# Four pairs instead of three by seven products in the second part's down, and an earlier product with A12, in a decoder block's feed-forward networks

## The chip, the cores and the metric

The kernel runs on one core of a Trainium2 chip, in one launch. The metric is the device time of that launch in microseconds (us). Engines are named as in the profile: TensorE (PE, with its weight loads as PEld), VectorE (DVE), ScalarE (ACT), GpSimd (POOL) and SyncE (SP).

## The reference

One block of a hybrid decoder for 256 tokens, model width 2048, in float32. Cut to what matters here:

```python
def swiglu(x, w_gu, w_down):
    gate, up = jnp.split(x @ w_gu, 2, axis=-1)
    return (jax.nn.silu(gate) * up) @ w_down

h = h + 0.5 * swiglu(rms_norm(h, ffn1_norm), ffn1_w_gu, ffn1_w_down)
h = h + hybrid_mixer(rms_norm(h, mix_norm), ...)
h = h + 0.5 * swiglu(rms_norm(h, ffn2_norm), ffn2_w_gu, ffn2_w_down)
gate = jax.nn.sigmoid(rms_norm(h, ple_norm) @ ple_w_gate)
h = h + gate * (p @ ple_w_proj)
return rms_norm(h, final_norm)
```

The hidden width of both feed-forward networks (FFN1 and FFN2) is 5632. The change touches these two alone.

## The kernel before, in words

**Products of two numbers each.** Every matrix product is taken in float32r with operands split in two, a high part and a low one: high by high, high by low, low by high, so three matmuls of 128 x 128 by 512 columns where one would stand. A weight arrives as `raw`; ScalarE casts it (`whi`, L77) and VectorE subtracts (`wlo`, L78). A "pair" is 256 rows of weights by 512 columns, with three buffers for `whi` and `wlo` and four for `raw`. `next_weights` (L82 to L96) runs two pairs and one weight sum ahead of TensorE.

**Parts and groups.** An FFN has its 5632 hidden columns in eleven blocks of 512, in parts of three, four and four blocks (`PARTS`). A part runs one group for the gate and up of each of its blocks (banks g0, g1, u0, u1), and then two down groups, each for two of the four output blocks (banks d0, d1, d0, d1). A down group of part two or three has eight pairs for each output block, and part one's has six.

**Seven products.** A part of each group's pairs, `ns` of them, isn't multiplied plainly (L550 to L552) but by Strassen and Winograd's scheme: with 2 x 2 blocks, the input's A11 to A22 and the weights' quarters, seven products of sums take the place of eight. A pair costs 24 matmuls plainly in a group and 21 by seven products (`product`, L324 to L352: 3 x `ns` matmuls in each of the seven, L342 to L344). The tuple `NS_DOWN` holds `ns` for the down groups of the three parts, 2, 3 and 3 before; `NS` is 4 for gate and up.

- Weight quarters lie in four buffers named R, loaded by a queue of GpSimd (L279). Sums of quarters are made by VectorE (`add`, L307) or by a load that adds (`add_loaded`, L314). Each product's weights are cast by ScalarE (`shi`, L298) and subtracted by VectorE (`slo`, L299); `shi` and `slo` have **two buffers** each. Their width is 512 x `ns`: 1536 elements at three pairs, 2048 at four.
- Input sums come from `halves` (L420 to L471): VectorE adds high and low (S, L456), makes four sums (L462), ScalarE casts (Sh, L464), VectorE subtracts (Sl, L465). Products 0, 4 and 6 take A11, A12 and A22 as they are and need none of it.
- Products 0 and 1 end with a copy of their bank on ScalarE (L347), products 2 and 3 with a copy (`part`, L350) and a subtraction on VectorE (L352).

**The order.** `plan` (L362 to L412) lays the seven products of a group between the plain pairs of the group ahead of it, beginning behind the second or third pair, one product for each further pair. The order of the seven is `SEVEN`, 0, 1, 2, 4, 3, 5, 6; the prediction counts by place, so that "the fifth product" is the fifth one in that order. The work beside the matmuls (`down_input`, L473 to L505: gate by up, a transposition by VectorE and a trip through memory, the cast hTh L504 and the subtraction hTl L505) goes in steps behind each pair (`lanes`). The tile scheduler has the last word on the order on each engine, so a product may come apart and stand between plain matmuls.

Of the kernel before, what the change touches and what calls it, by code (L numbers as in the profile page):

```python
# [27 lines left out]


NS = 4  # L30
NS_DOWN = tuple(3 if i1 - i0 == 4 else 2 for i0, i1 in PARTS)


SEVEN = (0, 1, 2, 4, 3, 5, 6)


W_IN_ORDER = (2, 0, 4, 3, 1, 5, 8, 10, 12, 9, 11, 13, 6, 7)
# [9 lines left out]
def block_kernel(ctx, tc, a, out):  # L47
# [15 lines left out]
    lanes = Lanes(4)  # L63
# [184 lines left out]
    class Group:  # L248
# [8 lines left out]
        def __init__(self, kind, part, src, quarters, ns, bank, nb=0):  # L257
            self.kind, self.part, self.src, self.ns, self.nb, self.bank = kind, part, src, ns, nb, bank
            self.quarters, self.raw, self.first = quarters, {}, False
            self.last = part == len(PARTS) - 1  # L260
            self.banks = self.follower = None
            self.plain = [(b, g) for b in range(2) for g in range(ns, len(src[0]))]
            if kind == "dn" and nb == 0:

                self.plain.sort(key=lambda x: x[1] >= len(src[0]) - 2)
            elif kind == "behind":

                self.plain.sort(key=lambda x: x[1] // 2)
            self.sums = self.all_sums()
# [20 lines left out]
        def all_sums(self):  # L290

            fp = current[0]

            def halved(j, b):
                w = self.raw[j, b]
                hi = fp.tile([P, NS, NB], F32R, tag="shi", name="shi", bufs=2)[:, 0:self.ns]
                lo = fp.tile([P, NS, NB], F32R, tag="slo", name="slo", bufs=2)[:, 0:self.ns]
                keep(nc.scalar.copy(hi, w))  # L298
                nc.vector.tensor_tensor(out=lo, in0=w, in1=hi, op=ALU.subtract)  # L299
                return hi, lo  # L300

            def keep(ins):

                return tc.keep_in_program_order(ins) if self.first == "2" else ins

            def add(x, y):
                keep(nc.vector.tensor_tensor(out=self.raw[x], in0=self.raw[x], in1=self.raw[y], op=ALU.add))  # L307

            def add_loaded(x, y):


                if self.first:
                    return add(x, y)
                nc.gpsimd.dma_start(out=self.raw[x], in_=self.quarters[y[1]][y[0]], accum_op=ALU.add)  # L314

            for i in SEVEN:
                ws = halved(*((0, 0), (0, 0), (0, 0), (0, 1), (1, 0), (1, 1), (0, 0))[i])
                if i == 0:
                    add((0, 0), (0, 1))
                    add_loaded((0, 1), (1, 1))  # L320
                elif i == 1:
                    add((0, 0), (1, 1))
                elif i == 2:
                    add_loaded((0, 0), (1, 0))  # L324
                yield ws
# [28 lines left out]
    def plan(n):  # L354
# [9 lines left out]
        for p, (i0, i1) in enumerate(PARTS):  # L364
            for i in range(i0, i1):
                plain = PLAIN[n]
                if i < plain:
                    src = [([a[f"w_gu{n}0"][2 * i + b][g] for g in range(KD // 2)], None) for b in range(2)]
                else:
                    src = [sources("w_gu" + n, 2 * (i - plain) + b) for b in range(2)]  # L370
                groups.append(Group("gu", p, [x[0] for x in src], [x[1] for x in src], NS if i >= plain else 0,
                                    len(groups) % 2))
            for nb in (0, 2):
                src = [sources(f"w_down{n}{p}", nb + b) for b in range(2)]
                groups.append(Group("dn", p, [x[0] for x in src], [x[1] for x in src], NS_DOWN[p], len(groups) % 2, nb))
        if n == "2":
            src = [sources("w_behind", b) for b in range(2)]
            groups.append(Group("behind", len(PARTS), [x[0] for x in src], [x[1] for x in src], NS_BEHIND,
# [44 lines left out]
    def halves(kind, his, los, ns, wait=0, at_once=2):  # L423
# [19 lines left out]
        for g0 in range(0, ns, at_once):  # L443
            n = min(at_once, ns - g0)
            k0 = 2 * (g0 % 2)
            hi, lo = (x[g0 // 2][:, k0:k0 + 2 * n] for x in (his, los))
            keep = lambda ins: ins
            if g0 == 2 and n == 1:

                keep = tc.keep_in_program_order  # L450
                yield
            if n == 2:
                x = fp.tile([P, 2 * NB], F32, tag="sil", name="S")
            else:
                x = act.tile([P, NB], F32, tag="nat", name="S", bufs=4)
            keep(nc.vector.tensor_tensor(out=x, in0=hi.bitcast(F32).rearrange("p k x -> p (k x)"),  # L456
                                         in1=lo.bitcast(F32).rearrange("p k x -> p (k x)"), op=ALU.add))
            xv = x.rearrange("p (g j t y) -> p g j t y", g=n, j=2, t=2)
            a11, a12, a21, a22 = (xv[:, :, j, t, :] for t in range(2) for j in range(2))
            for o, y, z, op in ((a22, a21, a22, ALU.subtract), (a21, a11, a21, ALU.subtract),  # L460
                                (a11, a22, a11, ALU.subtract), (a12, a11, a12, ALU.add)):
                nc.vector.tensor_tensor(out=o, in0=y, in1=z, op=op)  # L462
            sx = [y[:, g0:g0 + n].rearrange("p g j t y -> p (g j t y)") for y in (sh, sl)]
            nc.scalar.copy(sx[0], x)  # L464
            nc.vector.tensor_tensor(out=sx[1], in0=x, in1=sx[0], op=ALU.subtract)  # L465
            if not g0 % 2 + n == 1 or g0 + n == ns:
                yield

    def ffn(n, nT, r, scale, next_norm, stat):
        xs = picker(*nT)  # L470
        late = callable(r)  # L471
        with tc.tile_pool(name="ffn", bufs=1) as fp:
# [43 lines left out]
            for group, todo in ffn_plan[n]:  # L516
# [5 lines left out]
                if dn and group.nb and not group.last:  # L522
                    lanes.add(1, halves("gu", *nT, NS))
                elif dn and group.nb and group.follower:
                    lanes.add(1, halves("behind", *nxt, NS_BEHIND, 4))
                elif not dn and group.follower.kind == "dn" and not group.part:
                    lanes.add(1, halves("dn", hTh[i0:], hTl[i0:], NS_DOWN[group.part]))
                if dn and group.last and nxt is None:
                    nxt = new_nT()
                if group.banks is None:  # L530
# [1 line left out]
                for kind, one in todo:  # L532
                    if kind == "seventh":
                        follower = group.follower
                        follower.product(SEVEN[one])
                        if group.part and not dn and one == 5 and follower.kind == "gu" and \
                                follower.follower.kind == "dn":
                            p = PARTS[group.part][0]
                            lanes.add(1, halves("dn", Later(hTh, p), Later(hTl, p), NS_DOWN[group.part], 0, 1))
                        continue  # L540
                    b, g = one
                    whi, wlo = next_weights()
# [29 lines left out]
                    else:  # L572
# [7 lines left out]
                        hTl.append(tl)  # L580
                        i0, i1 = PARTS[group.part]

                        last = (3 if i1 - i0 == 4 else 2) if len(hTh) == i1 else 0
                        gen = down_input(outs, sil, th, tl, last)
                        next(gen)

# [762 lines left out]
def _layout(i):  # L1349
    f = {k: np.asarray(v) for k, v in i.items()}  # L1350
    m = {}
# [5 lines left out]
    for n in "12":  # L1357
# [4 lines left out]
        _parted(m, f"w_gu{n}", b[2 * PLAIN[n]:], NS)  # L1362
        b = _blocks(f[f"ffn{n}_w_down"][0])
        for p, (i0, i1) in enumerate(PARTS):
            _parted(m, f"w_down{n}{p}", b[:, 2 * i0:2 * i1], NS_DOWN[p])
    _parted(m, "w_behind", _blocks(f["ple_w_gate"][0])[0:2], NS_BEHIND)
    w = f["w_in"][0]
    m["w_in"] = _blocks(np.concatenate([w[:, :4096], w[:, 4112:]], axis=1))
# [29 lines left out]
```

## Time and profile before

| | us |
|---|---|
| three runs, median | 1944.74 (1944.4 to 1944.83) |
| the profiled execution | 1945.28 |
| its span, first to last instruction | 1943.6 |
| TensorE busy in it | 1928.1 (99%) |
| VectorE busy | 1570.4 (81%) |
| ScalarE busy | 1164.1 (60%) |
| granted TensorE clock, mean | 0.999 |

In a group's row stand line, engine, operation and tile, the shape, the count, then busy time and mean ns of one, then the idle time of the engine just ahead of it with what ended most of it. In a row of the waits stand the waiting instruction, what it waited for, the sum, the times and the longest. In a row of the timeline stand start, duration, engine, line and instruction. A matmul's record runs from issue to its end and overlaps the next one's.

### The profile page before, as it was taken

Reading aid. Unit: us, or ns where it says so; the run is one execution under the profiler, and the core shown is the slowest. Engines: PE = TensorE matmul, PEld = TensorE weight load, DVE = VectorE, ACT = ScalarE, POOL = GpSimd, SP = SyncE. Lnnn points to the kernel's source line nnn. Section 1 sums busy time; section 2 is a strip of 40 time slices with the busy share of each in tenths; the row PEclk is TensorE's granted clock in tenths of the full one; section 3 lists DMA queues with packets and bytes.
Section 4 is the critical chain, followed back from the end, with each engine's and each line's share of the span. In section 5 each row is a group of like instructions: output and inputs, shape, how many; then the busy total and the mean of one; then the engine's idle time right before and its main releaser. Section 6 shows DMA issues by size and latency. Waiting matters only on the chain.

```text
span 1943.6 us, 24163 instructions
## 1 busy us (share of the span) xinstructions
PE 1928.1 (99%) x8884; PEld 1594.0 (82%) x8884; DVE 1570.4 (81%) x1703; ACT 1164.1 (60%) x1362; POOL 148.4 (8%) x226
## 2 busy tenths in 40 slices
PE   9999999999999999999999999999999999999998
PEld 7888888888888888878788888888888888888886
DVE  7879878997789766797856579899888987888865
ACT  6656666666666557664555456566556755657654
POOL 0010110000010000010100000010000100001000
PEclk9999999999999999999999999999999999999999
DMA  8778898888888765556565776788888987989764
GB/s 307 269 236 282 252 293 285 237 288 249 280 285 242 228 218 171 176 169 211 161 213 159 244 283 231 226 281 289 248 275 241 327 264 244 271 237 314 234 214 143
DMA packets 144182, 475.05 MB, mean 244 GB/s; under 512 B 19648, under 2 KB 47296, under 8 KB 129856
## 3 DMA queue, kind: packets, MB, share of 16 engines
q1 hardware_dynamic: 107200, 302.16, 44.4%
q0 software_dynamic: 25920, 160.44, 30.2%
q10 hardware_dynamic: 10944, 10.91, 1.8%
q8 instruction: 69, 1.13, 0.2%
q14 instruction: 49, 0.40, 0.1%
HBM read 451.44 MB, written 22.02 MB: 244 GB/s over the span
## 4 chain that ended last, share of the span: by engine, by line
PE 92%; DVE 5%; DMA 2%; issue 1%; ACT 0%; POOL 0%; SPq 0%; POOLq 0%; DVEq 0%; ACTq 0%
PE d L550 5%; PE d L552 5%; PE d L551 5%; PE u L551 5%; PE u L552 5%; PE u L550 5%; PE g L343 5%; PE g L342 5%; PE g L344 5%; PE g L551 4%; PE g L552 4%; PE pj L112 4%; PE pj L113 4%; PE pj L114 4%; PE g L550 4%; PE d L344 3%
## 5 line engine op out<-in xcount | busy, mean ns | idle before, releaser
L77 ACT CAST whi<-raw 128x1024 fp32r<-128x1024 f32 (+1 forms) x489 | 511.3, 1049 | 401.1 <-PE pj L114 106.6
L78 DVE TENSOR_TENSOR wlo<-raw,whi 128x1024 fp32r<-128x1024 f32 (+1 forms) x489 | 592.0, 1218 | 162.9 <-ACT whi L77 161.8
L299 DVE TENSOR_TENSOR slo<-R,shi 128x2048 fp32r<-128x2048 f32 (+2 forms) x224 | 444.9, 1989 | 132.1 <-ACT shi L298 130.1
L298 ACT CAST shi<-R 128x2048 fp32r<-128x2048 f32 (+2 forms) x224 | 373.9, 1671 | 141.5 <-DVE R L307 62.7
L112 PE MATMUL pj<-whi,nTh 128*128 128x512 f32 x448 | 179.4, 401 | 0.0
L113 PE MATMUL pj<-wlo,nTh 128*128 128x512 f32 x448 | 175.2, 391 | 1.1 <-DVE wlo L78 1.1
L114 PE MATMUL pj<-whi,nTl 128*128 128x512 f32 x448 | 174.9, 390 | 0.0
L550 PE MATMUL d<-whi,hTh 128*128 128x512 f32 x448 | 174.5, 390 | 0.0
L551 PE MATMUL d<-wlo,hTh 128*128 128x512 f32 x448 | 174.4, 389 | 0.0
L552 PE MATMUL d<-whi,hTl 128*128 128x512 f32 x448 | 173.4, 389 | 0.0
L551 PE MATMUL g<-wlo,nTh 128*128 128x512 f32 x400 | 156.6, 391 | 0.6 <-DVE wlo L78 0.6
L552 PE MATMUL g<-whi,nTl 128*128 128x512 f32 x400 | 156.0, 390 | 0.0
L551 PE MATMUL u<-wlo,nTh 128*128 128x512 f32 x400 | 155.8, 389 | 0.2 <-DVE wlo L78 0.2
L552 PE MATMUL u<-whi,nTl 128*128 128x512 f32 x400 | 155.6, 389 | 0.0
L550 PE MATMUL g<-whi,nTh 128*128 128x512 f32 x400 | 155.0, 391 | 0.6 <-ACT nTh L161 0.6
L550 PE MATMUL u<-whi,nTh 128*128 128x512 f32 x400 | 153.4, 389 | 0.0
L307 DVE TENSOR_TENSOR R<-R 128x2048 f32<-128x2048 f32 (+2 forms) x68 | 135.7, 1996 | 0.1
L113 PEld LDWEIGHTS pj<-wlo,nTh 128*128 128x128 f32 x448 | 84.2, 188 | 18.9 <-DVE wlo L78 2.7
L550 PEld LDWEIGHTS d<-whi,hTh 128*128 128x128 f32 x448 | 84.1, 188 | 18.1 <-ACT hTh L504 1.0
L552 PEld LDWEIGHTS d<-whi,hTl 128*128 128x128 f32 x448 | 84.1, 188 | 17.8
L114 PEld LDWEIGHTS pj<-whi,nTl 128*128 128x128 f32 x448 | 84.1, 188 | 17.6
L551 PEld LDWEIGHTS d<-wlo,hTh 128*128 128x128 f32 x448 | 84.1, 188 | 17.4
(332 smaller groups left out, 3447.0 us busy)
## 6 DMA issues: line engine op xcount, KB each, us to landing
raw<-in_w_gu SPq DMA_DIRECT2D x199, 512.0 KB, 5.8
raw<-in_w_down SPq DMA_DIRECT2D x112, 512.0 KB, 6.4
raw<-in_w_in SPq DMA_DIRECT2D x112, 512.0 KB, 3.4
R<-in_w_gu2q POOLq DMA_DIRECT2D x54, 1024.0 KB, 8.6
R<-in_w_gu1q POOLq DMA_DIRECT2D x48, 1024.0 KB, 8.3
raw<-in_w_out SPq DMA_DIRECT2D x32, 512.0 KB, 4.3
tT<-scr SPq DMA_DIRECT2D x22, 512.0 KB, 5.8
R<-in_w_down11q POOLq DMA_DIRECT2D x12, 768.0 KB, 7.0
```

The source lines that it names most:

```text
L77: nc.scalar.copy(hi[:, j, :], raw[:, j, :])
L78: nc.vector.tensor_tensor(out=lo[:, j, :], in0=raw[:, j, :], in1=hi[:, j, :], op=ALU.subtract)
L112: nc.tensor.matmul(outs[t], xh[:, c], whi[:, j, :], start=st, stop=False)
L113: nc.tensor.matmul(outs[t], xh[:, c], wlo[:, j, :], start=False, stop=False)
L114: nc.tensor.matmul(outs[t], xl[:, c], whi[:, j, :], start=False, stop=sp)
L298: keep(nc.scalar.copy(hi, w))
L299: nc.vector.tensor_tensor(out=lo, in0=w, in1=hi, op=ALU.subtract)
L307: keep(nc.vector.tensor_tensor(out=self.raw[x], in0=self.raw[x], in1=self.raw[y], op=ALU.add))
L344: nc.tensor.matmul(out, xl, whi[:, g, :], start=False, stop=sp, skip_group_check=True)
L550: nc.tensor.matmul(out, xh[:, c], whi[:, j, :], start=st, stop=False, skip_group_check=True)
L551: nc.tensor.matmul(out, xh[:, c], wlo[:, j, :], start=False, stop=False, skip_group_check=True)
L552: nc.tensor.matmul(out, xl[:, c], whi[:, j, :], start=False, stop=sp, skip_group_check=True)
```

## The change

`NS_DOWN` gets a number for each of the two down groups of a part: (2, 2), (4, 4) and (3, 3). So both down groups of part two, in both FFNs, take four of their eight pairs by seven products instead of three; the weights in memory are laid out to match (one array for each group). `SEVEN_DOWN` is a second order, 0, 4, 1, 2, 3, 5, 6, used where the first down group of parts two and three follows the last gate and up: the product with A12, number 4, comes second instead of fourth. The steps of `halves` and `down_input` are fitted to four pairs.

```diff
...
 
 
 NS = 4
-NS_DOWN = tuple(3 if i1 - i0 == 4 else 2 for i0, i1 in PARTS)
+NS_DOWN = (2, 2), (4, 4), (3, 3)
 
 
 SEVEN = (0, 1, 2, 4, 3, 5, 6)
+SEVEN_DOWN = (0, 4, 1, 2, 3, 5, 6)
 
 
 W_IN_ORDER = (2, 0, 4, 3, 1, 5, 8, 10, 12, 9, 11, 13, 6, 7)
...
         def __init__(self, kind, part, src, quarters, ns, bank, nb=0):
             self.kind, self.part, self.src, self.ns, self.nb, self.bank = kind, part, src, ns, nb, bank
             self.quarters, self.raw, self.first = quarters, {}, False
+            self.seven = SEVEN_DOWN if kind == "dn" and part and nb == 0 else SEVEN
             self.last = part == len(PARTS) - 1
             self.banks = self.follower = None
             self.plain = [(b, g) for b in range(2) for g in range(ns, len(src[0]))]
...
                     return add(x, y)
                 nc.gpsimd.dma_start(out=self.raw[x], in_=self.quarters[y[1]][y[0]], accum_op=ALU.add)
 
-            for i in SEVEN:
+            for i in self.seven:
                 ws = halved(*((0, 0), (0, 0), (0, 0), (0, 1), (1, 0), (1, 1), (0, 0))[i])
                 if i == 0:
                     add((0, 0), (0, 1))
...
                 groups.append(Group("gu", p, [x[0] for x in src], [x[1] for x in src], NS if i >= plain else 0,
                                     len(groups) % 2))
             for nb in (0, 2):
-                src = [sources(f"w_down{n}{p}", nb + b) for b in range(2)]
-                groups.append(Group("dn", p, [x[0] for x in src], [x[1] for x in src], NS_DOWN[p], len(groups) % 2, nb))
+                src = [sources(f"w_down{n}{p}{nb // 2}", b) for b in range(2)]
+                groups.append(Group("dn", p, [x[0] for x in src], [x[1] for x in src], NS_DOWN[p][nb // 2],
+                                    len(groups) % 2, nb))
         if n == "2":
             src = [sources("w_behind", b) for b in range(2)]
             groups.append(Group("behind", len(PARTS), [x[0] for x in src], [x[1] for x in src], NS_BEHIND,
...
             k0 = 2 * (g0 % 2)
             hi, lo = (x[g0 // 2][:, k0:k0 + 2 * n] for x in (his, los))
             keep = lambda ins: ins
-            if g0 == 2 and n == 1:
+            if g0 >= 2 and n == 1:
 
                 keep = tc.keep_in_program_order
-                yield
+                if g0 == 2:
+                    yield
             if n == 2:
                 x = fp.tile([P, 2 * NB], F32, tag="sil", name="S")
             else:
...
                 elif dn and group.nb and group.follower:
                     lanes.add(1, halves("behind", *nxt, NS_BEHIND, 4))
                 elif not dn and group.follower.kind == "dn" and not group.part:
-                    lanes.add(1, halves("dn", hTh[i0:], hTl[i0:], NS_DOWN[group.part]))
+                    lanes.add(1, halves("dn", hTh[i0:], hTl[i0:], NS_DOWN[group.part][0]))
                 if dn and group.last and nxt is None:
                     nxt = new_nT()
                 if group.banks is None:
...
                 for kind, one in todo:
                     if kind == "seventh":
                         follower = group.follower
-                        follower.product(SEVEN[one])
+                        follower.product(follower.seven[one])
                         if group.part and not dn and one == 5 and follower.kind == "gu" and \
                                 follower.follower.kind == "dn":
                             p = PARTS[group.part][0]
-                            lanes.add(1, halves("dn", Later(hTh, p), Later(hTl, p), NS_DOWN[group.part], 0, 1))
+                            lanes.add(1, halves("dn", Later(hTh, p), Later(hTl, p), NS_DOWN[group.part][0], 0, 1))
                         continue
                     b, g = one
                     whi, wlo = next_weights()
...
                         hTl.append(tl)
                         i0, i1 = PARTS[group.part]
 
-                        last = (3 if i1 - i0 == 4 else 2) if len(hTh) == i1 else 0
+                        last = (6 - NS_DOWN[group.part][0] if i1 - i0 == 4 else 2) if len(hTh) == i1 else 0
                         gen = down_input(outs, sil, th, tl, last)
                         next(gen)
 
...
         _parted(m, f"w_gu{n}", b[2 * PLAIN[n]:], NS)
         b = _blocks(f[f"ffn{n}_w_down"][0])
         for p, (i0, i1) in enumerate(PARTS):
-            _parted(m, f"w_down{n}{p}", b[:, 2 * i0:2 * i1], NS_DOWN[p])
+            for j in range(2):
+                _parted(m, f"w_down{n}{p}{j}", b[2 * j:2 * j + 2, 2 * i0:2 * i1], NS_DOWN[p][j])
     _parted(m, "w_behind", _blocks(f["ple_w_gate"][0])[0:2], NS_BEHIND)
     w = f["w_in"][0]
     m["w_in"] = _blocks(np.concatenate([w[:, :4096], w[:, 4112:]], axis=1))
```

The rows below are those of FFN1's part two, in program order, with a number behind each tile's name. Lines in the changed kernel are one to five higher than before.

VectorE between the second and the third product, before: `slo_2728` is the second product's, `slo_2793` the third's, `R` the quarter sums, `sil` to `tb` the transposition, `S` input sums, and `wlo` plain pairs of the last gate and up.

```order
L299 TENSOR_TENSOR slo_2728<-R_2548,shi_2727 128x1536
L487 STREAM_TRANSPOSE tb_2744<-sil_2526 128x4x128
L307 TENSOR_TENSOR R_2548<-R_2548,R_2625 128x1536
L487 STREAM_TRANSPOSE tb_2744<-sil_2526 128x4x128
L78 TENSOR_TENSOR wlo_2749<-raw_2747,whi_2748 128x1024
L456 TENSOR_TENSOR S_2770<-hTh_2382,hTl_2383 128x512
L299 TENSOR_TENSOR slo_2793<-R_2548,shi_2792 128x1536
L462 TENSOR_TENSOR S_2770<-S_2770 128x128
L78 TENSOR_TENSOR wlo_2799<-raw_2797,whi_2798 128x1024
```

And now, where `slo_2728` is the product with A12:

```order
L301 TENSOR_TENSOR slo_2728<-R_2633,shi_2727 128x2048
L491 STREAM_TRANSPOSE tb_2743<-sil_2526 128x4x128 x2
L79 TENSOR_TENSOR wlo_2748<-raw_2746,whi_2747 128x1024
L460 TENSOR_TENSOR S_2769<-hTh_2382,hTl_2383 128x512
L301 TENSOR_TENSOR slo_2803<-R_2548,shi_2802 128x2048
L466 TENSOR_TENSOR S_2769<-S_2769 128x128
L309 TENSOR_TENSOR R_2548<-R_2548,R_2625 128x2048
L466 TENSOR_TENSOR S_2769<-S_2769 128x128
L79 TENSOR_TENSOR wlo_2809<-raw_2807,whi_2808 128x1024
```

The wide addition of R has moved behind the third product's slo, ahead of the last row's wlo.

ScalarE at the fourth to seventh products, before (d0 and d1 are banks, `shi_2974` is the first product of the second down group, the others are the first group's):

```order
L298 CAST shi_2825<-R_2633 128x1536
L350 COPY part_2859<-d1_2779 128x512
L298 CAST shi_2862<-R_2584 128x1536
L77 CAST whi_2902<-raw_2901 128x1024
L77 CAST whi_2940<-raw_2939 128x1024
L77 CAST whi_2960<-raw_2959 128x1024
L298 CAST shi_2895<-R_2625 128x1536
L350 COPY part_2930<-d1_2779 128x512
L298 CAST shi_2933<-R_2548 128x1536
L298 CAST shi_2974<-R_2866 128x1536
L504 CAST hTh_2701<-tT_2919 128x4x4x32 x2
```

And now, with `shi_2876` the fifth product, `shi_2915` the sixth, `shi_2956` the seventh and `shi_3000` the first of the second down group:

```order
L468 CAST Sh_2683<-S_2777 128x512
L349 COPY d1_2788<-d0_2787 128x512
L300 CAST shi_2876<-R_2584 128x2048
L352 COPY part_2912<-d1_2786 128x512
L300 CAST shi_2915<-R_2625 128x2048
L78 CAST whi_2983<-raw_2982 128x1024
L78 CAST whi_3035<-raw_3034 128x1024
L352 COPY part_2953<-d1_2786 128x512
L300 CAST shi_2956<-R_2548 128x2048
L300 CAST shi_3000<-R_2880 128x2048
L508 CAST hTh_2701<-tT_2939 128x4x4x32 x2
```

The copy of the bank d0 stands ahead of the fifth product's cast, and two wide casts stand behind each other at the end.

TensorE at the first product of the second down group (bank `d1_3061`), before: the rows ahead of it are plain pairs of the first down group, and 16 rows lie between the end of the seventh product (`shi_2933`) and the second group's first.

```order
L551 MATMUL d1_2779<-wlo_2941,hTh_2382 128x512
L552 MATMUL d1_2779<-whi_2940,hTl_2383 128x512
L550 MATMUL d0_2778<-whi_2960,hTh_2701 128x512
L551 MATMUL d0_2778<-wlo_2961,hTh_2701 128x512
L550 MATMUL d1_2779<-whi_2960,hTh_2701 128x512
L551 MATMUL d1_2779<-wlo_2961,hTh_2701 128x512
L342 MATMUL d1_3061<-shi_2974,hTh_2085 128x512
L343 MATMUL d1_3061<-slo_2975,hTh_2085 128x512
L344 MATMUL d1_3061<-shi_2974,hTl_2086 128x512
```

And now (bank `d1_3090`), with `shi_2915` the sixth product and `shi_2956` the seventh:

```order
L346 MATMUL d0_2787<-shi_2915,Sl_2684 128x512
L344 MATMUL d0_2787<-shi_2915,Sh_2683 128x512
L345 MATMUL d0_2787<-slo_2916,Sh_2683 128x512
L346 MATMUL d0_2787<-shi_2915,Sl_2684 128x512
L344 MATMUL d1_2786<-shi_2956,hTh_2085 128x512
L344 MATMUL d1_3090<-shi_3000,hTh_2085 128x512
L345 MATMUL d1_2786<-slo_2957,hTh_2085 128x512
L346 MATMUL d1_2786<-shi_2956,hTl_2086 128x512
L344 MATMUL d1_2786<-shi_2956,hTh_2085 128x512
L345 MATMUL d1_2786<-slo_2957,hTh_2085 128x512
L346 MATMUL d1_2786<-shi_2956,hTl_2086 128x512
```

The first matmul of the second group stands one matmul behind the end of the sixth product, inside the seventh; the rest of that product follows behind the seventh.

## The prediction

> **What bounds the kernel now.** I read the page's busy times first, then the chain that ended last, then all that TensorE waited for.
>
> ```profile
> span 1943.6 us, 24163 instructions
> PE 1928.1 (99%) x8884; PEld 1594.0 (82%) x8884; DVE 1570.4 (81%) x1703; ACT 1164.1 (60%) x1362; POOL 148.4 (8%) x226
> PE 92%; DVE 5%; DMA 2%; issue 1%; ACT 0%; POOL 0%; SPq 0%; POOLq 0%; DVEq 0%; ACTq 0%
> PE g L551 <- DVE wlo L78: 0.6, 2, 0.4
> PE u L343 <- DVE slo L299: 0.3, 1, 0.3
> PE u L551 <- DVE wlo L78: 0.2, 1, 0.2
> ```
>
> TensorE is the bound. In the FFNs its waits for weights come to 1.1 us in all, so a matmul that goes is a gain in full, and a weight that comes late is a loss in full. The price of a matmul comes from a stretch without a wait:
>
> ```profile
> 300.16 0.39 PE L550 MATMUL g<-whi,nTh 128*128 128x512 f32 x1
> ...
> 304.92 0.39 PE L550 MATMUL g<-whi,nTh 128*128 128x512 f32 x1
> ```
>
> In the kernel's order these two are 21 matmuls apart, and 4.76/21 = 0.2267 us. The record's 0.39 is one matmul from issue to end.
>
> Last I looked at the stretch the change touches, part two's down of FFN1. The windows show, in this order, the pass from gate/up to the first down group, from there to the second, and on to the next gate/up (columns: window and its length, PE, PEld, DVE, ACT, POOL busy, clock, DMA share, GB/s):
>
> ```profile
> 337.00:376.00 39.00, 39.00 (x173) 32.06 (x172) 35.30 (x43) 23.79 (x27) 3.96 (x6) 1.00 0.80 239
> 376.00:413.00 37.00, 37.00 (x165) 30.61 (x165) 35.14 (x34) 25.19 (x26) 3.96 (x6) 1.00 0.97 322
> 413.00:451.00 38.00, 38.00 (x168) 31.06 (x167) 34.87 (x31) 21.26 (x18) 2.88 (x4) 1.00 0.81 244
> ```
>
> VectorE is idle there for 3.70, 1.86 and 3.13 us only, and the DMA engines are at 0.97 in the middle. TensorE never waits, but its cover is thin.
>
> **The change part by part.** Prices of what grows and of what goes (groups, with the mean ns of one behind the busy time):
>
> ```profile
> L299 DVE TENSOR_TENSOR slo<-R,shi 128x2048 fp32r<-128x2048 f32 x133 | 304.4, 2290 | 112.7 <-ACT shi L298 111.9 <-DMA raw<-in_w_gu 0.6
> L299 DVE TENSOR_TENSOR slo<-R,shi 128x1536 fp32r<-128x1536 f32 x56 | 97.9, 1754 | 10.3 <-ACT shi L298 10.1
> L307 DVE TENSOR_TENSOR R<-R 128x2048 f32<-128x2048 f32 x42 | 95.7, 2280 | 0.1
> L307 DVE TENSOR_TENSOR R<-R 128x1536 f32<-128x1536 f32 x16 | 27.9, 1746 | 0.0
> L78 DVE TENSOR_TENSOR wlo<-raw,whi 128x1024 fp32r<-128x1024 f32 x487 | 590.6, 1220 | 160.2 <-ACT whi L77 159.1
> L298 ACT CAST shi<-R 128x2048 fp32r<-128x2048 f32 x133 | 254.3, 1913 | 104.1 <-DVE R L307 53.7 <-PE g L344 27.2 <-PE u L344 21.2
> L298 ACT CAST shi<-R 128x1536 fp32r<-128x1536 f32 x56 | 83.0, 1482 | 21.9 <-PE d L344 8.4 <-PE g L344 6.8 <-PE u L344 6.7
> ```
>
> *1. Matmuls.* Four down groups (two per FFN) take one pair more by seven products: each loses 24 plain matmuls and gains 21. That is 4 x 3 = 12 fewer, 12 x 0.2267 = **-2.72 us**. The Trainium skill ("TensorE: Matmul & The Clock Gate", Part 1, on the 56 ns gap) has 215.7 ns between warm matmuls of 512 columns; by it the gain would be 2.59; the trace's 226.7 decides.
>
> Eight raw pairs go too (per FFN four subtractions, 4.9 us of VectorE). What comes per FFN: 14 wide slo for narrow ones, 14 x 0.536 = 7.5, four wide adds, 4 x 0.534 = 2.1, and one more set of input sums, about 2.5 by its rows:
>
> ```profile
> L462 DVE TENSOR_TENSOR S<-S 128x128 f32<-128x128 f32 x48 | 12.9, 290 | 0.1
> L456 DVE TENSOR_TENSOR S<-hTh,hTl 128x512 f32<-128x512 f32 x12 | 8.3, 688 | 0.0
> L465 DVE TENSOR_TENSOR Sl<-S,Sh 128x512 fp32r<-128x512 f32 x12 | 8.3, 691 | 2.7 <-ACT Sh L464 2.7
> ```
>
> (four of the first, one of each other.) So VectorE takes on 7.2 us net per FFN in a stretch with 8.7 us idle. Averages don't say what is late; the single hand-overs do. These show how fast one engine follows another:
>
> ```profile
> 374.46 0.39 PE L344 MATMUL d<-shi,Sl 128*128 128x512 f32 x1
> 374.88 1.49 ACT L298 CAST shi<-R 128x1536 fp32r<-128x1536 f32 x1 [2.12 <-PE d L344]
> ...
> 370.80 0.59 ACT L350 COPY part<-d 128x512 f32<-128x512 f32 x1 [0.78 <-PE d L344]
> 371.28 1.48 ACT L298 CAST shi<-R 128x1536 fp32r<-128x1536 f32 x1
> 372.80 1.76 DVE L299 TENSOR_TENSOR slo<-R,shi 128x1536 fp32r<-128x1536 f32 x1 [0.27 <-ACT shi L298]
> ```
>
> ScalarE starts 0.03 to 0.04 behind a matmul's end (374.85), a copy holds it 0.48 before the next cast, VectorE starts 0.04 behind the cast. Products have two shi and two slo buffers: a product's cast waits for the last matmul of the product two before it. With ns at four, this chain grows by 0.43 + 0.54.
>
> *2. The pair behind the third product* (its wlo is used at 357.23 in before):
>
> ```profile
> 337.23 1.76 DVE L299 TENSOR_TENSOR slo<-R,shi 128x1536 fp32r<-128x1536 f32 x1 [0.50 <-ACT shi L298]
> 338.91 0.29 DVE L462 TENSOR_TENSOR S<-S 128x128 f32<-128x128 f32 x1
> ...
> 352.21 1.19 DVE L78 TENSOR_TENSOR wlo<-raw,whi 128x1024 fp32r<-128x1024 f32 x1
> 355.78 1.23 DVE L78 TENSOR_TENSOR wlo<-raw,whi 128x1024 fp32r<-128x1024 f32 x1
> ```
> ```profile
> 353.45 0.50 PE L551 MATMUL g<-wlo,nTh 128*128 128x512 f32 x1
> 357.23 0.39 PE L551 MATMUL u<-wlo,nTh 128*128 128x512 f32 x1
> ```
>
> VectorE starts an instruction 0.08 before the record ahead ends (338.91 against 338.99), and works without a gap of note from 337.23 to 357.01. In the changed order it has ahead of that wlo three wide slo and two wide adds (3 x 0.536 + 2 x 0.534), an input sum of 0.60 fewer and one of 0.20 more: +2.28. Its start moves by the wider cast, 0.43. So the wlo ends at 359.72 and TensorE could go on at 359.77. TensorE gets there nine matmuls later, 2.04, less the 0.11 by which its record at 353.45 is longer than 0.39 (a wait that goes): 359.16. Wait **0.61** (0.2 to 0.8, by what VectorE makes up).
>
> *3. The fifth product.* Its cast waits for the third product's last matmul, and ScalarE copies a bank first: 0.39 + 0.04 + 0.48 + 1.91 + 0.04 + 2.29 + 0.05 to the matmul (353.40 to 353.45 in the rows above) = 5.20. TensorE has 17 matmuls between, 3.85. Wait **1.35** (0.87 if the copy goes behind the cast). This counts from a matmul, so an earlier wait gives it no relief.
>
> *4. The sixth product.* VectorE does a wide slo, a subtraction of a bank and a wide slo, 2.20 + 0.61 = 2.81 apart, for 12 matmuls, 2.72: **0.1** (0 to 0.3).
>
> *5. The first product of the second down group.* One of its matmuls now stands behind the first matmul of the seventh product. Its cast waits for the sixth product's last matmul: 0.39 + 0.04 + 1.91 + 0.05 = 2.39, against two matmuls, 0.45. Wait **1.94**. Were its cover there, the seventh's slo would still be late: it has the chain of step 3 and 15 matmuls, 5.20 - 3.40 = 1.80. So I take 1.94 (1.8 to 1.94).
>
> *6. The rest* (the last block's hidden input to the down pairs, the input sums of the next gate/up): **0.3** (0 to 0.6), an estimate halfway between nothing and the 0.6 us that g's waits for a wlo come to above. On ScalarE that block's cast and the whi of the next pairs are queued behind the waiting casts of step 5.
>
> *7. What goes.* Of the 1.1 us of waits in the FFNs I count half, **-0.6** (0 in the high end): those at 353.45 and its like in FFN2, and at part three, where the product with A12 needs no input sum and so VectorE's work ahead of the second product shrinks. Late next, where they go, is step 2's wlo. Nothing else in part three changes; its price is within 0.3 us in all.
>
> *Loads.* One load of a weight quarter for the second down group now starts behind the fifth product's slo:
>
> ```profile
> R<-in_w_gu1q POOLq DMA_DIRECT2D x48, 1024.0 KB, 8.3
> ```
>
> It is wanted by the addition behind the second group's first slo: 24 matmuls (5.44), the waits of steps 4 and 5 (2.04) and a slo (2.20) later, 9.68, so it lands 1.4 us ahead. I cost it at nothing; those waits are its cover, and what a landing in the 0.97 stretch takes beyond 1.4 us is rival D.
>
> Per FFN 0.61 + 1.35 + 0.1 + 1.94 + 0.3 = 4.30, twice 8.60. Net 8.60 - 2.72 - 0.6 = +5.28. The profiled execution took 1945.28 us (1943.6 of it span), 0.54 over the median of the runs, so its like would take 1950.6; against the median, 1944.74, it is **1950.0**. By the low ends: 2 x (0.2 + 0.87 + 1.8) - 3.32 = +2.4, 1947.2; by the high ends 2 x 4.99 - 2.72 = +7.3, 1952.0.
>
> **The rivals.**
>
> *B, one large wait is not there.* A buffer comes free sooner, or a cast slips ahead, so that step 5 or step 3 falls. For it: ScalarE is busy for only 23.79 of 39 us. Against: it is held by a buffer, not by work, and behind step 5's wait the seventh's slo is late anyway. Without step 5 the time is 1950.0 - 3.88 = 1946.1, without step 3 1950.0 - 2.70 = 1947.3.
>
> *C, not slower.* The product with A12 needs no input sum, so VectorE does not have to make one for the second product; if this gives it a lead of over 1.35 us (step 3's shortfall) that lasts to the end of part two, the waits of steps 2 to 5 dissolve and the twelve matmuls alone count: 1944.74 - 2.72 - 0.6 = 1941.4. For it: VectorE idles 3.70 us in the first window. Against: steps 3 and 5 start at a matmul's end, and a lead on VectorE does not move them.
>
> *D, the loads are late too.* The wide quarters land in the stretch at 0.97 DMA share; if the quarter of the second down group or a raw pair comes 1 to 1.7 us past its need, each FFN loses that beside the sum: 1952.0 to 1953.4, and with a second such wait up to 1957. For it: the share, and the margin of 1.4 us. Against: fewer raw pairs are fetched.
>
> *E, full records in line.* If VectorE's instructions followed each other by whole records, step 2 would have some 25 hand-overs of 0.085, 2.1 us more, per FFN: 1950.0 + 4.2 = 1954.2. The overlap at 338.91 speaks against it. The Trainium skill ("VectorE: DVE Perf Modes", The DRAIN you can't avoid) says that the next operation does not start until the pipe is empty; in this trace it starts 0.08 before the record's end.
>
> *F, it does not do what it says.* In part three only the order changes, and no matmul goes; that it does nothing there is within step 7's 0.3 us and moves no chance.
>
> **How the numbers follow.** About 0.2%, 3.9 us, is what a measurement of this kernel can tell from no change: under 1940.85 is faster, over 1948.63 slower. Forecast 0.62 with its own range 1947.2 to 1952.0, of which 0.06 lie under 1948.63; B 0.18; C 0.08, of which 0.02 under 1940.85; D 0.11; E 0.01. Faster 0.02; same 0.06 + 0.18 + 0.06 = 0.30; slower 0.56 + 0.11 + 0.01 = 0.68. The range runs from 1945.0 to 1956.0: it leaves out C and some of D's end, 0.08 + 0.04, and a little of B.
>
> **What would show it.** In the changed profile: 12 matmuls fewer; in each FFN a wait of 1.9 us at the first product of the second down group, put down to ScalarE's shi (or to VectorE's slo, 1.8); one of 1.3 at the fifth product for its slo; one of 0.6 for a wlo some 22 us after part two's switch begins; DMA not named among the releasers. The prediction is wrong if TensorE's waits for weights in the FFNs sum to under 3 us, if they stand at other instructions, or if a raw or quarter load is what ends them.

## The result and the profile after

The changed kernel took **1952.11 us** (median of seven runs, 1950.22 to 1954.37), the kernel before 1944.83 (seven runs, 1944.01 to 1945.21): a ratio of 1.0039, interval 1.0028 to 1.0051. It is slower by 7.3 us, where 5.3 was forecast.

The page of the changed kernel, span and busy times:

```profile
span 1950.7 us, 24126 instructions
...
PE 1929.0 (99%) x8872; PEld 1591.1 (82%) x8872; DVE 1585.3 (81%) x1707; ACT 1169.7 (60%) x1356; POOL 148.4 (8%) x226
```

TensorE has 12 matmuls fewer and a span 7.1 us longer. A share of 99% doesn't show that; the waits do. All that TensorE waited for in the FFNs (waiting line, releaser, sum, times, longest):

```profile
PE d L344 <- ACT shi L300: 3.5, 2, 1.8
PE d L345 <- DVE slo L301: 2.2, 2, 1.1
...
PE u L555 <- DVE wlo L79: 1.0, 2, 0.5
...
PE g L555 <- DVE wlo L79: 0.6, 2, 0.4
PE g L554 <- ACT nTh L162: 0.5, 1, 0.5
PE u L345 <- DVE slo L301: 0.3, 1, 0.3
```

The first three are new, two times each: once per FFN. The last three were there before. Where the new ones stand, in FFN1's timeline of TensorE, with the instruction behind each:

```profile
359.43 0.50 PE L555 MATMUL u<-wlo,nTh 128*128 128x512 f32 x1 [0.49 <-DVE wlo L79]
359.77 0.39 PE L556 MATMUL u<-whi,nTl 128*128 128x512 f32 x1
...
374.34 0.40 PE L556 MATMUL u<-whi,nTl 128*128 128x512 f32 x1
375.85 0.50 PE L345 MATMUL d<-slo,Sh 128*128 128x512 f32 x1 [1.11 <-DVE slo L301]
376.18 0.40 PE L346 MATMUL d<-shi,Sl 128*128 128x512 f32 x1
...
381.05 0.39 PE L346 MATMUL d<-shi,Sl 128*128 128x512 f32 x1
381.27 0.39 PE L344 MATMUL d<-shi,hTh 128*128 128x512 f32 x1
383.42 0.50 PE L344 MATMUL d<-shi,hTh 128*128 128x512 f32 x1 [1.76 <-ACT shi L300]
383.76 0.39 PE L345 MATMUL d<-slo,hTh 128*128 128x512 f32 x1
```

What is lost is read from start to start: 375.85 - 374.34 = 1.51 for a step that otherwise takes 0.23, so 1.28, though the bracket says 1.11, because the record of the matmul ahead goes on for 0.40. In the same way 383.42 - 381.27 - 0.23 = 1.92. The matmul behind each wait is late again: 0.34 instead of 0.23 (383.42 to 383.76), 0.11 more.

ScalarE ahead of the long wait (its timeline):

```profile
378.66 0.59 ACT L352 COPY part<-d 128x512 f32<-128x512 f32 x1 [1.01 <-PE d L346]
379.14 1.92 ACT L300 CAST shi<-R 128x2048 fp32r<-128x2048 f32 x1
381.47 1.90 ACT L300 CAST shi<-R 128x2048 fp32r<-128x2048 f32 x1 [0.41 <-PE d L346]
```

The cast for the second group's first product has idle time ahead of it: it waited for TensorE to finish the sixth product and free the buffer, and then TensorE waited for the cast. That is the loop of step 5.

### The profile page after: what moved, and what is told of

Its sections match the earlier page's. It is cut to its first block, busy times and chain, and to the rows that moved or that the text cites. A ratio compares the mean times of both kernels' runs of the same rounds, so it can differ in the third digit from the quotient of the medians.

```text
span 1950.7 us, 24126 instructions
## 1 busy us (share of the span) xinstructions
PE 1929.0 (99%) x8872; PEld 1591.1 (82%) x8872; DVE 1585.3 (81%) x1707; ACT 1169.7 (60%) x1356; POOL 148.4 (8%) x226
## 4 chain that ended last, share of the span: by engine, by line
PE 91%; DVE 5%; DMA 1%; issue 1%; ACT 1%; POOL 0%; SPq 0%; POOLq 0%; DVEq 0%; ACTq 0%
PE d L554 5%; PE d L555 5%; PE d L556 5%; PE u L555 5%; PE u L556 5%; PE g L345 4%; PE g L344 4%; PE g L346 4%; PE u L554 4%; PE pj L113 4%; PE pj L114 4%; PE pj L115 4%; PE g L555 4%; PE g L556 4%; PE g L554 4%; PE d L345 3%
## 5 line engine op out<-in xcount | busy, mean ns | idle before, releaser
L78 ACT CAST whi<-raw 128x1024 fp32r<-128x1024 f32 (+1 forms) x481 | 503.3, 1050 | 388.8 <-PE pj L115 110.0
L79 DVE TENSOR_TENSOR wlo<-raw,whi 128x1024 fp32r<-128x1024 f32 (+1 forms) x481 | 582.2, 1216 | 160.8 <-ACT whi L78 159.3
L301 DVE TENSOR_TENSOR slo<-R,shi 128x2048 fp32r<-128x2048 f32 (+2 forms) x224 | 459.8, 2054 | 126.7 <-ACT shi L300 124.7
L300 ACT CAST shi<-R 128x2048 fp32r<-128x2048 f32 (+2 forms) x224 | 386.1, 1725 | 164.1 <-DVE R L309 91.8
L554 PE MATMUL d<-whi,hTh 128*128 128x512 f32 x416 | 162.0, 391 | 0.0
L555 PE MATMUL d<-wlo,hTh 128*128 128x512 f32 x416 | 161.6, 389 | 0.0
L556 PE MATMUL d<-whi,hTl 128*128 128x512 f32 x416 | 160.9, 389 | 0.0
L113 PEld LDWEIGHTS pj<-whi,nTh 128*128 128x128 f32 x448 | 84.2, 188 | 16.6
L554 PEld LDWEIGHTS d<-whi,hTh 128*128 128x128 f32 x416 | 78.1, 188 | 17.7 <-ACT hTh L508 1.6
L556 PEld LDWEIGHTS d<-whi,hTl 128*128 128x128 f32 x416 | 78.1, 188 | 16.5
```

The lines of the kernel that those rows point to most:

```text
L78: nc.scalar.copy(hi[:, j, :], raw[:, j, :])
L79: nc.vector.tensor_tensor(out=lo[:, j, :], in0=raw[:, j, :], in1=hi[:, j, :], op=ALU.subtract)
L113: nc.tensor.matmul(outs[t], xh[:, c], whi[:, j, :], start=st, stop=False)
L554: nc.tensor.matmul(out, xh[:, c], whi[:, j, :], start=st, stop=False, skip_group_check=True)
L555: nc.tensor.matmul(out, xh[:, c], wlo[:, j, :], start=False, stop=False, skip_group_check=True)
L556: nc.tensor.matmul(out, xl[:, c], whi[:, j, :], start=False, stop=sp, skip_group_check=True)
```

## The experiments

All times are medians beside runs of the kernel before on the same chip (1944.73 for the first four, 1944.44 for the next four, 1944.63 for the last four).

**1 and 2: the two parts of the change apart.** Four pairs with the old order:

```diff
-SEVEN_DOWN = (0, 4, 1, 2, 3, 5, 6)
+SEVEN_DOWN = SEVEN
```

> Four pairs in both halves of part two's down, with the old order of the seven products everywhere. Theory (two buffers for shi and slo are too few for products of four pairs that stand back to back): the order of the products matters little, the waits move to other products but stay; by the program's order 1.6 us at the fourth and fifth products, 1.8 at the sixth's slo, 0.5 at the rest, about 3.9 per FFN, so 1944.8 - 2.7 + 7.8 = 1950 or more. Rival (the early product with A12 brings the waits): without it only the twelve matmuls count, 1942.

Measured 1959.06, 1.0075 (1.0062 to 1.0087). Its longest waits in the FFNs:

```profile
PE d L344 <- ACT shi L300: 3.4, 4, 1.1
PE d L345 <- DVE slo L301: 3.3, 2, 1.6
PE d L344 <- ACT Sh L468: 2.8, 2, 1.5
PE g L555 <- DVE wlo L79: 2.7, 4, 1.2
PE d L554 <- ACT hTh L508: 1.9, 1, 1.9
```

The rival falls: without the early A12 the loss is 14.3 us, twice as large. But "the order matters little" falls too. shi and slo are waited for as expected; on top come an input sum (Sh) and a wlo ahead of it, since the product in second place needs a sum then, and VectorE has to make it.

The early A12 with three pairs:

```diff
-NS_DOWN = (2, 2), (4, 4), (3, 3)
+NS_DOWN = (2, 2), (3, 3), (3, 3)
```

> The product with A12 second, with three pairs as before. Theory: no product stands back to back with another one, no new wait for shi or slo; 1944.8 less up to 0.6, so 1944.2 to 1944.8. Rival (the order brings the waits): 1948 or more.

Measured 1945.54 (1943.56 to 1947.7), 1.0002 (0.9994 to 1.0011): no change that can be told. Its profile has no wait for a slo or shi of part two. It has something else, of which the kernel before shows none: ScalarE waits for loads into weight quarters (the third part's loads that add, 120q in FFN1 and 220q in FFN2, among them), and TensorE waits for the last block's hTl at 626.58 and 1769.71 us, where part three passes to down:

```profile
PE d L556 <- DVE hTl L509: 1.4, 2, 0.7
```
```profile
ACT shi L300 <- DMA R<-in_w_down120q: 2.0, 1, 2.0
ACT shi L300 <- DMA R<-in_w_down220q: 1.8, 1, 1.8
```

**3 and 4: one down group alone.** Four pairs in the first group, three in the second:

```diff
-NS_DOWN = (2, 2), (4, 4), (3, 3)
+NS_DOWN = (2, 2), (4, 3), (3, 3)
```

> Four pairs in the first of part two's two down groups only, three in the second: six matmuls fewer. Theory: the fifth product waits as in the changed kernel (1.3 per FFN), the wlo of step 2 too (0.65), and the second group's first product waits for a narrow cast, 0.39 + 0.04 + 1.48 + 0.05 - 0.45 = 1.5; with 0.1 behind each wait some 3.9 per FFN: 1944.8 - 1.4 + 7.8 - 0.6 = 1950.6, and 1.8 more in an FFN where the clock falls. Rival (the second group's width makes the waits): about 1943.5.

Measured 1953.88, 1.0046 (1.0033 to 1.0058). The wait at the second group's first product, in its timeline:

```profile
382.76 0.50 PE L344 MATMUL d<-shi,hTh 128*128 128x512 f32 x1 [1.32 <-ACT shi L300]
```

1.32 and the 0.17 of the record are 1.5, as worked out with the narrow cast's 1.48 in the wide one's place. The time is 9.1 over before, not 5.8. Its profile shows one piece that the expectation hadn't, 1.1 us of waits for hTl where part three passes to down, as in experiment 2, and 0.6 of the miss is step 7's, which the expectation took off again; the rest stays open.

The other way round, with the input sums made for four pairs:

```diff
-NS_DOWN = (2, 2), (4, 4), (3, 3)
+NS_DOWN = (2, 2), (3, 4), (3, 3)
-halves("dn", ..., NS_DOWN[group.part][0], ...)
+halves("dn", ..., max(NS_DOWN[group.part]), ...)
```

> Four pairs in the second of part two's two down groups only; the input sums are made for four pairs. Six matmuls fewer. Theory: by the program's order plain pairs stand between the products, so no shi or slo is late; 1944.8 - 1.4 = 1943.4, up to 1 more or less for a wlo. Rival (more VectorE work in the stretch is what costs, wherever the products stand): half of the changed kernel's loss, 1948.

Measured 1943.37 (1941.48 to 1945.74), 0.9996 (0.9987 to 1.0005): 1.4 us under before, as six matmuls would have it, but within what can't be told from no change. Its profile shows no wait for a shi or slo of a down group. The second group's width brings no such wait; the first group's does, and the wait at the second group's first product is the first group's doing, since its sixth and seventh products stand back to back.

**5 and 6: when a buffer comes free.** The same memory in four half buffers, for the changed kernel and, as a control, for the one before:

```diff
-hi = fp.tile([P, NS, NB], F32R, tag="shi", name="shi", bufs=2)[:, 0:self.ns]
-lo = fp.tile([P, NS, NB], F32R, tag="slo", name="slo", bufs=2)[:, 0:self.ns]
+for g0 in range(0, self.ns, 2):
+    m = min(2, self.ns - g0)
+    hi = fp.tile([P, 2, NB], F32R, tag="shi", name="shi", bufs=4)[:, 0:m]
+    lo = fp.tile([P, 2, NB], F32R, tag="slo", name="slo", bufs=4)[:, 0:m]
...
```

> The changed kernel with shi and slo in four buffers of two pairs each instead of two of four, the same memory: a buffer comes free when half a product is done. Each cast and subtraction of over two pairs becomes two instructions, which costs VectorE and ScalarE about 0.15 to 0.2 us more for each product. Theory (the waits come from when buffers come free): the waits at the fifth product and at the second group's first product go, though VectorE has more to do; against the same edit of the kernel before 2.7 us faster, 1942 if the edit alone costs nothing. Rival (VectorE's work is the cause): waits as in the changed kernel or longer, 1952 or more.

> The kernel before with the same four half buffers: the control. Theory: 1944 to 1946, since its buffers were never late and VectorE's added work is mostly hidden. Rival (VectorE's work is the cause): 1948 or more.

Measured 1955.44, 1.0058 (1.0045 to 1.0071), and for the control 1952.26, 1.0045 (1.0031 to 1.0058). In time both miss. The edit by itself costs 7.8 us in the kernel before, in waits at other places that its own scheduling brings (for a hidden input 2.4, a wlo 2.0, an input sum 1.9). The waits of the two steps are gone all the same: in the changed kernel with half buffers TensorE waits for nothing from 337 to 451 us, and in FFN2's stretch, 1478 to 1600, only for these:

```profile
PE u L560 <- DVE wlo L79: 1.1, 1, 1.1
PE d L351 <- DVE hTl L514: 0.4, 1, 0.4
```

Against its control it is still 3.2 us slower by the medians, not 2.7 faster, though the two intervals overlap. Its profile has waits that the control hasn't:

```profile
PE d L561 <- DVE hTl L514: 2.7, 2, 1.8
```

These stand at 630 and 1780 us, where part three passes to down. Experiments 2, 3, 7 and 8 have the same wait there with whole buffers, so it isn't the half buffers' doing (the point on loads below takes it up).

Nor do half buffers alone explain why the waits of steps 3 and 5 are gone, for the edit changed the order on TensorE too. Twelve matmuls of plain pairs now stand between the sixth and the seventh product, where the changed kernel has none (381.05 and 381.27 above):

```profile
379.76 0.39 PE L351 MATMUL d<-shi,Sl 128*128 128x512 f32 x1
379.99 0.39 PE L559 MATMUL u<-whi,nTh 128*128 128x512 f32 x1
...
382.71 0.39 PE L349 MATMUL d<-shi,hTh 128*128 128x512 f32 x1
```

Twelve matmuls take 2.72 us, more than either reading of step 5's wait. So the experiment doesn't tell an earlier free buffer from more cover. What ties the wait of step 5 to the chain are the rows of the changed kernel, and experiments 3 and 8, which change one term of the chain (3) or its cover (8) and get the wait worked out for it. Step 3's chain is checked by the size of its wait alone, 1.1 by the profile in the changed kernel and in experiments 3, 7, 8 and 9.

**7: the clock.** In the changed kernel's profile the granted clock fell in FFN2, right behind the 1.92 us loss at that place (windows: stretch and length, busy times, granted clock, DMA share, GB/s):

```profile
1524.00:1530.20 6.20, 4.45 (x19) 3.22 (x18) 6.04 (x6) 5.10 (x5) 1.05 (x2) 1.00 0.96 388
1530.20:1533.90 3.70, 3.70 (x10) 2.85 (x10) 3.70 (x3) 0.23 (x1) 0.00 (x1) 0.54 0.88 308
1533.90:1536.00 2.10, 2.10 (x11) 1.71 (x10) 2.10 (x4) 1.03 (x1) 0.88 (x1) 1.00 0.11 39
```

```profile
1530.29 0.63 PE L344 MATMUL d<-shi,hTh 128*128 128x512 f32 x1
1530.72 0.63 PE L345 MATMUL d<-slo,hTh 128*128 128x512 f32 x1
```

Seven matmuls start 0.43 behind the one ahead instead of 0.23, and an eighth 0.39: 1.6 us. FFN1's wait, of the same length, did not do it; the last section shows what differs. The edit fills the wait:

```diff
+if i == 6 and self.kind == "dn" and self.part == 1 and self.nb == 0:
+    for _ in range(8):
+        nc.tensor.matmul(out[0:64, :], fill.bitcast(F32R), whi[:, 0, :], start=False, stop=False,
+                         skip_group_check=True)
```

> The changed kernel with eight matmuls that add zero (64 columns of zeros) put ahead of the seventh product of part two's first down group, where TensorE waits 1.9 us. Theory of the clock (a wait of 1.8 us lets the granted clock fall to half for 3.5 us in some executions, 1.8 us each): TensorE doesn't stop, no slice at half clock, each run near the fastest of the changed kernel, 1950.0 with a spread under 1 us. Rival (the clock falls by itself): mean 1952 and spread 4 us as in the changed kernel. If the 1.9 us were not a wait but work on TensorE's path, eight matmuls would add 1.8 per FFN, 1955.

Measured 1952.17 (1950.27 to 1953.89), 1.0040 (1.0028 to 1.0053). In its timeline of FFN1 and its windows around the place in both FFNs:

```profile
380.94 2.01 PE L343 MATMUL d<-shi,fill 128*64 128x512 f32 x8
382.78 0.82 PE L348 MATMUL d<-shi,hTh 128*128 128x512 f32 x2
```
```profile
378.00:389.00 11.00, 11.00 (x49) 8.21 (x48) 10.83 (x10) 6.00 (x6) 1.54 (x3) 1.00 0.81 317
1524.00:1536.00 12.00, 12.00 (x53) 9.02 (x52) 11.84 (x9) 6.66 (x7) 1.60 (x3) 1.00 0.81 304
```

Eight matmuls fitted in without a cost: TensorE was idle there. The clock stays at 1.00 in both, and yet median and spread are those of the changed kernel. My theory that the clock makes the spread falls, at least as the whole of it.

**8: the place of one matmul.** The second group's first product is kept behind the seventh on TensorE:

```diff
+keep = (tc.keep_in_program_order if self.kind == "dn" and self.part == 1 and
+        (i == 6 and self.nb == 0 or i == 0 and self.nb) else lambda x: x)
-nc.tensor.matmul(out, xh, whi[:, g, :], start=st, ...)
+keep(nc.tensor.matmul(out, xh, whi[:, g, :], start=st, ...))
```

> The changed kernel with the second group's first product kept behind the seventh product of the first group on TensorE. Theory: the cast of the second group's first product is no longer waited for, but the seventh's slo is late in its place: 5.20 us behind the fifth product's last matmul against 14 matmuls, 3.17, a wait of 2.0; time as the changed kernel, 1950 to 1954. Rival (only the place of that one matmul costs): 2 x 1.9 less, 1946 to 1948.

Measured 1956.37, 1.0064 (1.0052 to 1.0077). In its timeline the wait has changed hands:

```profile
384.00 0.51 PE L347 MATMUL d<-slo,hTh 128*128 128x512 f32 x1 [1.77 <-DVE slo L301]
```

1.77 and 0.17 are 1.94, for 2.0 expected: the seventh's slo is late in the cast's place. Behind it a new wait came, for the last block's hTl: 1.6 us in each FFN's part two, the largest piece of the 4 us more (the third of the three stands in part three, as in experiment 2):

```profile
PE d L558 <- DVE hTl L511: 4.1, 3, 1.6
```

**9 to 12: part three's order.** After the second experiment I took part three's late loads for the rest of the loss.

```diff
-self.seven = SEVEN_DOWN if kind == "dn" and part and nb == 0 else SEVEN
+self.seven = SEVEN_DOWN if kind == "dn" and part == 1 and nb == 0 else SEVEN
```

> The changed kernel with the old order of the seven products in part three, so that the product with A12 is second in part two alone. Theory (what the changed kernel loses beyond the waits in part two, and its spread of 4 us, comes from part three: the load that adds, issued behind the fourth product instead of the third, lands late, the seventh's cast waits for it, and the last block's hTl is queued behind): no ScalarE wait for a load in part three, runs near the fastest of the changed kernel, 1950.2, spread 2 us or less. Rival (the clock falling behind the 1.9 us wait makes the spread): median 1952, spread 4 us.

Measured 1952.30 (1951.36 to 1954.59), 1.0041 (1.0027 to 1.0055). ScalarE waits for no quarter's load any more, and the time is the changed kernel's: as an account of the median, this theory falls too. Its profile has instead a wait of 0.5 for an hTl at 1495.08 us, which the changed kernel's profile hasn't.

The same with part == 2 and three pairs everywhere:

> The kernel before with the product with A12 second in part three alone; three pairs throughout. Theory (part three's load that adds lands late): ScalarE waits for that load of the third part and the time is 0 to 2 us over before, 1945.5, spread 3 to 4 us. Rival (no effect): 1944.6, spread as before.

Measured 1945.41 (1943.63 to 1948.36), 1.0006 (0.9997 to 1.0015): not to be told from no change, with a spread of 4.7 us in eleven runs.

The last two have four pairs in the second group alone (as experiment 4), with the early A12 in part two only, and with the old order everywhere:

> Four pairs in the second of part two's down groups only, the product with A12 second in part two alone. Theory: six matmuls fewer and none of part three's late loads: 1944.6 - 1.4 = 1943.2 or a little less, with a smaller spread than with the early A12 in part three (1941.5 to 1945.7). Rival (part three's order costs nothing): the same as with it, 1943.4.

> Four pairs in the second of part two's down groups only, the old order of the seven products everywhere; six matmuls fewer. Theory: the second group's products have plain pairs between them and no shi is late; 1944.6 - 1.4 = 1943.2, spread as before. If the second group's width alone brings waits for shi or slo: 1945 or more.

Measured 1943.17 (1942.22 to 1944.94), 0.9992 (0.9983 to 1.0001), and 1942.92 (1942.45 to 1943.56), 0.9992 (0.9983 to 1.0001). The latter is 1.7 us under before, near six matmuls' 1.4. Both intervals just reach 1, so neither is shown to beat the kernel before. Over eleven runs each, the spread is 4.3 us in experiment 4, 2.7 in experiment 11 and 1.1 in experiment 12; that the early A12 in part three widens it is likely by this, but not shown, since the kernel before spreads by 4.0 over the 27 runs beside the last two. TensorE's waits for weights and input in the FFNs of the last one are those of the kernel before and no other:

```profile
PE g L555 <- DVE wlo L79: 0.7, 2, 0.5
PE g L554 <- ACT nTh L162: 0.4, 1, 0.4
PE u L345 <- DVE slo L301: 0.3, 1, 0.3
```

## Why the prediction was right, point by point

- **Step 1, right in the count.** x8872 after x8884. Experiments 4 and 12 give 1.4 and 1.7 us for half of it, by medians, for 1.36 worked out, but neither is clear of noise, and their profiles also lack a wait of 0.5 behind FFN2 that the kernel before has (below).
- **Step 2, right.** 0.61 forecast; 359.43 stands 0.65 late (0.49 and the 0.16 of the record ahead).
- **Step 3, right.** 1.35 forecast, 1.28 lost.
- **Step 4, right in being small.** No wait of the sixth product for its slo is in the list; the matmul behind its first with slo starts 0.07 late (378.98 instead of 378.91).
- **Step 5, right in size and in its reserve.** 1.94 forecast, 1.92 lost; experiment 8 put the seventh's slo in its place with 1.94. In experiment 5 both are gone, by half buffers and another order together.
- **Step 6, about right.** 0.3 forecast; one of the first down matmuls with the last block loses 0.22.
- **Step 7, wrong.** None of the listed waits for a wlo or slo was in this stretch. They lie where the kernel and the FFNs begin (10.6, 65 to 67 and 1170 us in before), the change touches none of these places, and 0.9 of the 1.1 us stand in the rows after as before (g 0.6, u 0.3). I took rows of a whole kernel for rows of the stretch without asking where they are. What did go is smaller: at 353.45 and three like places in before the next matmul starts 0.11 late, and in the changed kernel it doesn't. That is 0.4 of the 0.6 us.
- **A term that was left out.** Each wait delays the matmul behind it by a further 0.11: with four waits per FFN some 0.9 us in all.
- **Loads, as forecast for part two; part three was mis-sized**, "within 0.3 us". The early A12 there issues the last load that adds one product later, and the seventh product's cast can wait for it. The changed kernel's profiled execution was lucky: 0.2 us of that wait, and TensorE lost nothing. Other profiles with this order show what it can cost. Here is ScalarE's wait for 120q (FFN1) or 220q (FFN2), and what TensorE then loses at the last block's hTl, start to start:

| profile | FFN1: wait, lost | FFN2: wait, lost |
|---|---|---|
| changed kernel | none, 0 | 0.2, 0 |
| experiment 2 | 2.0, 0.91 | 1.8, 0.76 |
| experiment 3 | 1.6, 0.56 | 1.9, 0.88 |
| experiment 4 | none, 0 | none, 0 |
| experiment 7 | 1.4, 0.34 | 2.4, 1.40 |
| experiment 8 | 2.0, 0.99 | 0.8, 0 |
| experiment 10 | none, 0 | 1.2, 0.14 |

So about 1.0 us is covered, and the rest is lost in full. The profiles with whole buffers and the old order in part three (before, experiments 1, 9, 11 and 12) have neither wait. For experiment 7's loss:

```profile
ACT shi L300 <- DMA R<-in_w_down220q: 2.4, 1, 2.4
```
```profile
1777.42 0.39 PE L559 MATMUL d<-wlo,hTh 128*128 128x512 f32 x1
1779.05 0.50 PE L560 MATMUL d<-whi,hTl 128*128 128x512 f32 x1 [1.24 <-DVE hTl L513]
```

Four losses per FFN are 0.65 + 1.28 + 1.92 + 0.22 = 4.07 for the 4.30 of the sum; with 0.11 behind each, 4.5. Twice 4.5 less 2.72 is +6.3. The two profiled executions check this. From its first gate matmul to its last down matmul, FFN1 takes 686.91 us before and 689.91 after: with the 1.36 of six matmuls saved, 4.36 were lost. FFN2 takes 690.10 and 694.98, and there the fallen clock adds 1.6 to 1.7. Behind FFN2 the time falls by 0.8 (92.26 to 91.47), because a wait of before isn't there, which no step had in view:

```profile
PE gt L125 <- DVE wlo L78: 0.5, 1, 0.5
```

The two FFNs, this and 0.0 elsewhere make the 7.1 us of the spans. That a median of +7.3 lies so near is partly luck, since the clock and this wait were not in the sum. Among executions, the parts seen to vary are the clock, the loads of part three (0 to 1.4 us per FFN) and the wait at 1495 us; experiments 7 and 9, each without one of them, keep the median, so how they make up the spread of 4 us stays open.

Rivals: B didn't come (both large waits are there). C's mechanism is there in part, since the early A12 halves what four pairs lose (7.3 against 14.3), but no lead of VectorE moves a wait that starts at a matmul's end. D's place, a load in part two, doesn't show in the changed kernel: one wait of 0.2 for a load in part three is all. Late loads in part three, which no rival priced, cost other profiles up to 1.4 us per FFN. E's 2.1 us per FFN are not there.

## What to carry to other kernels

When the items of a two-buffer pipeline grow, work out the refill chain from the last use of the buffer (here 0.39 + 0.04 + 0.48 + 1.91 + 0.04 + 2.29 + 0.05) and compare it with the number of instructions that the final order really leaves in between; busy shares say nothing of it. If two chains end at one place, moving one only shows the other. Before a wait is booked as a gain, look up where in the kernel it stands. And read the order that an experiment really got: half buffers were meant to move one thing and moved two.

## What was not expected of the hardware

- **A clock that falls behind a wait of 1.9 us.** Eight matmuls start late, by up to 0.20 us each, granted clock 0.54, in one of two equal places of one execution. The Trainium skill ("TensorE: Matmul & The Clock Gate", Part 1) has the array at half clock after an idle window of about 3.4 us, with 426.7 ns between matmuls of 512 columns then. The spacing agrees with the 0.43 here; the idle time was much shorter than 3.4 us. The trace's clock record shows half clock for 3.41 us from 1530.20, behind 1525.76 us of full clock and ahead of 413.01 more: 447 and 121 times 3.413, so the clock changed on a grid of that step. On this grid the two places aren't equal. The step ahead of the fall has TensorE busy for less than half of it; in FFN1 the wait runs over the edge of a step, and the step that holds most of it is busy for more than half:

```profile
379.91:383.32 3.41, 1.75 (x8) 1.12 (x6) 3.31 (x3) 3.00 (x3) 0.00 (x0) 1.00 0.98 372
1526.79:1530.20 3.41, 1.66 (x7) 1.04 (x6) 3.25 (x3) 2.97 (x4) 0.53 (x1) 1.00 0.98 406
1530.20:1533.61 3.41, 3.41 (x9) 2.66 (x9) 3.41 (x3) 0.23 (x1) 0.00 (x1) 0.50 0.87 298
```

  Experiment 5's profile has a second such fall, 3.41 us from 1342.15, behind a step with 1.59 us busy. No other step that ends ahead of the last matmul, in any profile here, has a fall behind it or less than 1.7 us busy. The fall behind the last matmul, which every profile has, agrees: at once behind a step with 1.15 us busy in experiment 3, one step later where 1.71 were busy in the changed kernel. So a fall whenever a step is idle for more than half fits all of these traces; no run tested it.
- **A restart price.** The first matmul behind a wait has a record of 0.50 instead of 0.39, and the next one starts 0.34 later instead of 0.23, at each of the places shown.
